# A retention and DeltaNet layer on one core: gate weights in tiles of their own on POOL's queue, an early bias, x in 1 KB packets, a shorter end

## The chip, the core and the metric

The kernel runs on one core of a Trainium2 chip. The engines are PE (TensorE, matmuls), DVE (VectorE), ACT (ScalarE), POOL (GpSimd) and SP (SyncE, which here only issues DMA transfers); SP and POOL each own a queue of transfers, and 16 DMA engines serve both. The metric is device time in microseconds: the median of three runs was 3312.75 (3312.17 to 3316.98). A separately profiled execution gives the trace.

## The reference

One layer with two groups of heads, over 128 context tokens and 256 latent tokens, model width D = 4096, all in float32. Cut to what matters here (the mixer with its scans is left out):

```
mod = silu(c) @ w_ada + b_ada            # w_ada (4096, 3 * 4096)
shift, scale, gate = split(mod, 3)       # one row for the context, one for the latents
u = rms_norm(h, norm_w) * (1 + scale) + shift
out = mixer(u, ...)                      # u @ w_in, retention and gated delta rule, mixed @ w_out
h = h + gate * out
y = rms_norm(h, final_norm_w)
```

The change touches four places: loading x for the first norm, computing `gate`, loading w_out (4096 x 4096), and the last norm with its stores.

## The kernel before

The 384 tokens are three units of 128. A weight tile in fp32 is split into a high and a low part in a narrower float (`split_tile`): ACT casts it (L219, `wh`), DVE subtracts (L220, `wl`). A product is three matmuls: high x high, low x high, high x low (L270 to L272, L276 to L278).

**Start.** SP loads x in 16 blocks of 256 columns for three units, 48 transfers (`xload`, L485), between loads of w_ada. A block's tile holds two halves of 128 columns, each with three units side by side (L480), so a row of 256 columns lands in two places. ACT and DVE sum squares; `xnorm` makes the scale; `uprep` transposes x and applies scale and shift. Then the input projection starts, in stages.

**Middle.** Input projection and mixers, unchanged here. Of the 4096 gate columns, 2560 are computed there on PE.

**Output projection.** Eight groups of 512 columns, each 32 pieces of one 128-row block of w_out. w_out comes in tiles of two pieces from a ring of four (`raw`, RAW_RING), two transfers per tile (L207). The order of the program is written by `run_pieces`: it prepares pieces up to RING - 1 = 4 ahead of the one whose matmuls it writes, so casts and subtractions stand that far ahead on ACT and DVE; pieces of other kinds are written where they stand between.

Between the pieces of groups 1 to 6 stand those of `GateSum`: the last 1536 gate columns, four sums of 384 columns. A piece loads two 128-row blocks of w_ada into a tile of the same `raw` ring by SP (L352); DVE multiplies each block by silu(c) per row and adds it to two accumulators (L360, L362), one per kind of token; the second block's adds are put off behind the next split (`later`). At a sum's end PE adds over partitions (L382), the bias is read into an accumulator by POOL (L386), DVE adds (L388) and POOL writes gate rows to DRAM (L390).

For each group `pre`, five pieces before the group's end, has POOL read the gate rows (`go`, L1356), the last norm's weights (`wo`, L1357) and x (`xo`, L1359, three units), 1.5 MB in all. `rest` forms gate * out, adds x, multiplies by the norm's weight into `hw` and has ACT sum the squares (L1367 to L1372), small steps that are written between the next group's matmuls. The tiles of this stage come from a pool (`op`) that `open_out` opens near the end of group 0, when the mixers' pools are closed.

**End.** After a unit's last group `final` adds the eight sums, takes the inverse root on POOL, scales `hw` in four parts on DVE and ACT in turn (L1338, L1336), and SP stores each (L1339).

Each engine runs its instructions in the order in which they were written; so does each queue of transfers issue them.

Of the kernel before, what the change touches and what calls it, by code (L numbers as in the profile page):

```python
# [7 lines left out]
F32 = mybir.dt.float32  # L8
F32R = mybir.dt.float32r
AF = mybir.ActivationFunctionType  # L10
# [59 lines left out]
def hybrid_step(ctx: ExitStack, tc: tile.TileContext, x_prompt, x_sample, state_ret_fwd, state_ret_bwd,  # L70
# [129 lines left out]
    def load_piece(src, chunks, k0, nk, ring=None):  # L200
        shape = [128, nk, len(chunks), chunks[0][1]]
        if ring:
            raw = ring(shape)
        else:
            raw = wpool.tile(shape, F32, tag="raw", name="raw", bufs=RAW_RING)
        for i, (c0, cn) in enumerate(chunks):
            SP.dma_start(out=raw[:, :, i, :],  # L207
                         in_=src[k0 * 128:(k0 + nk) * 128, c0:c0 + cn].rearrange("(k p) n -> p k n", p=128))
        return raw

    later = []

    def split_tile(raw, shape, place=None):
        if place:
            h, lo = place
        else:
            h = wpool.tile(shape, F32R, tag="wh", name="wh", bufs=RING)
            lo = wpool.tile(shape, F32R, tag="wl", name="wl", bufs=RING)
        A.copy(h, raw)  # L219
        V.tensor_tensor(lo, raw, h.bitcast(F32), op=ALU.subtract)  # L220
        if later:
            later.pop(0)()
        return h, lo

    class Gemm:
# [115 lines left out]
    class GateSum:  # L341
# [3 lines left out]
        slots = 0.0  # L345

        def __init__(self, c0):
            self.c0 = c0
            self.pieces = [(self, i) for i in range(0, NK, 2)]

        def prepare(self, i):
            raw = load_piece(w_ada, [(2 * D + self.c0, GATE_W)], i, 2)  # L352
            if i == 0:
                self.acc = [oc["sb"].tile([128, GATE_W], F32, tag=f"ga{v}", name="gacc", bufs=2) for v in range(2)]

            def add(q):
                for v, acc in enumerate(self.acc):
                    w = cst[:, 2 * (i + q) + v:2 * (i + q) + v + 1]
                    if i + q == 0:
                        V.tensor_scalar(acc, raw[:, q, 0], scalar1=w, scalar2=None, op0=ALU.mult)  # L360
                    else:
                        V.scalar_tensor_tensor(out=acc, in0=raw[:, q, 0], scalar=w, in1=acc, op0=ALU.mult, op1=ALU.add)  # L362
            while later:
                later.pop(0)()
            add(0)
            if i + 2 < NK:
                later.append(lambda: add(1))
            else:
                add(1)

        def compute(self, i, hl):
            if i + 2 == NK:
                urgent.append(self.fin())
            return 1

        def fin(self):
            n, sb = GATE_W // 2, self.acc[0]
            parts = [(32 * q, q // 2, n * (q % 2)) for q in range(4)]
# [5 lines left out]
            for r, v, o in parts:  # L384
# [3 lines left out]
            V.tensor_tensor(sb[:, 0:n], ps, sb[:, 0:n], op=ALU.add)  # L388
            for r, v, o in parts:
                G.dma_start(out=d_gate[v:v + 1, self.c0 + o:self.c0 + o + n], in_=sb[r:r + 1, 0:n])  # L390
            clock["gate"] = self.c0 + GATE_W

    class Do:

# [921 lines left out]
    def open_out():  # L1316
        bg_drain()
        mx_ctx.close()
        mid_ctx.close()
        oc["sb"] = ctx.enter_context(tc.tile_pool(name="op", bufs=1))  # L1320
        oc["ps"] = ctx.enter_context(tc.tile_pool(name="ps_out", bufs=1, space=PSUM))
        oc["hw"] = oc["sb"].tile([128, 3, D], F32, name="hw")
        oc["sq"] = oc["sb"].tile([128, 3, 8], F32, name="sq")
        oc["rstd"] = oc["sb"].tile([128, 3], F32, name="rstd")

    def final(n):

        hw, r = oc["hw"], oc["rstd"][:, n:n + 1]
        V.tensor_reduce(r, oc["sq"][:, n], axis=AX.X, op=ALU.add)
        V.tensor_scalar(r, r, scalar1=1.0 / D, scalar2=EPS, op0=ALU.mult, op1=ALU.add)  # L1330
        power(r, r, 0)
        yield
        for i in range(4):
            cs = slice(1024 * i, 1024 * i + 1024)
            if i % 2:
                A.activation(hw[:, n, cs], hw[:, n, cs], AF.Copy, scale=r)  # L1336
            else:
                V.tensor_scalar(hw[:, n, cs], hw[:, n, cs], scalar1=r, scalar2=None, op0=ALU.mult)  # L1338
            SP.dma_start(out=y_unit[n][:, cs], in_=hw[:, n, cs])  # L1339
            if i % 2:  # L1340
                yield

    def out_done(c0):
        box = {}
        cs = slice(c0, c0 + 512)

        def pre():
            if not oc:
                open_out()
            bg_drain(("out", c0 - 512))  # L1350
            op = oc["sb"]
            assert clock["gate"] >= c0 + 512
            box["x"] = op.tile([128, 3, 512], F32, tag="xo", name="xo", bufs=1)
            box["g"] = op.tile([128, 2, 512], F32, tag="go", name="go")
            box["w"] = op.tile([128, 512], F32, tag="wo", name="wo")
            G.dma_start(out=box["g"], in_=d_gate[:, cs].partition_broadcast(128))  # L1356
            G.dma_start(out=box["w"], in_=final_norm_w[cs].partition_broadcast(128))  # L1357
            for m in range(3):
                G.dma_start(out=box["x"][:, m], in_=x_unit[m][:, cs])  # L1359

        def done(n, ps):
            bg_list.append((("out", c0), rest(n, ps)))

        def rest(n, ps):
            yield
            t = oc["sb"].tile([128, 512], F32, tag="to", name="to", bufs=3)
            V.tensor_tensor(t, ps, box["g"][:, min(n, 1)], op=ALU.mult)  # L1367
            yield
            V.tensor_tensor(t, t, box["x"][:, n], op=ALU.add)
            yield  # L1370
            V.tensor_tensor(oc["hw"][:, n, cs], t, box["w"], op=ALU.mult)
            A.activation(t, t, AF.Square, accum_out=oc["sq"][:, n, c0 // 512:c0 // 512 + 1])  # L1372
            yield
            if c0 + 512 == D:
                yield from final(n)
        return pre, done

# [83 lines left out]
```

## Time and profile before

| what | value |
|---|---|
| median of three runs | 3312.75 us |
| profiled execution, its own time | 3315.79 us |
| its span, first to last instruction | 3313.8 us |
| PE busy | 3217.4 us, 97% of the span |
| DVE busy | 1961.7 us, 59% |
| ACT busy | 1200.1 us, 36% |
| POOL busy | 302.3 us, 9% |
| mean granted clock of PE | 0.987 |
| read from HBM, written | 590.75 MB, 32.33 MB |

A busy PE is not PE at its peak: its instructions overlap, and 512-column matmuls follow each other every 0.23 us, or every 0.43 us where the granted clock is 0.5 (from 2825 us on, for one). Rows of the waits name the waiting engine, its tile and line, whom it waited for, and then the total in us, the number of waits and the longest. Rows of a timeline begin with start and duration in us; in brackets stands the idle time before, and what ended it. "x2" is a number of instructions. A row of DMA issues gives the size of one and the median time to its landing.

### The profile page before, as it was taken

The numbers are of one execution on the slowest core, as the hardware profiler recorded it, in microseconds if no ns is written. First come the engines' busy times: TensorE is split into PE (matmuls) and PEld (weight loads), VectorE is DVE, ScalarE is ACT, GpSimd is POOL, SyncE is SP. The second block draws the span as 40 slices with busy tenths as digits, with TensorE's granted clock in tenths as the row PEclk, the third lists the DMA queues.
The fourth block names the chain that finished last, engine by engine and source line by source line (L and its number), as shares of the span: only waits on it lengthen the run. The fifth ranks groups of instructions, "written<-read, shape, count | busy, mean of one in ns | idle before, by whom it ended". The sixth has DMA issues, their size and how long they took to land.

```text
span 3313.8 us, 51416 instructions
## 1 busy us (share of the span) xinstructions
PE 3217.4 (97%) x18948; PEld 2698.1 (81%) x18948; DVE 1961.7 (59%) x4065; ACT 1200.1 (36%) x2582; POOL 302.3 (9%) x484
## 2 busy tenths in 40 slices
PE   4999999999999999999999999999999999999998
PEld 2778888878799789789898789789789887787876
DVE  2554443336955746745856746756745855766774
ACT  3322222224345245235345245245245345223233
POOL 0000000001011011001011011011001012010001
PEclk7999999999999999999999999999999999999999
DMA  9998998984434644645445645644645445776665
GB/s 295 297 297 262 333 300 273 291 267 137 121 118 127 188 138 151 188 135 153 134 135 154 189 123 160 187 137 141 188 125 156 132 122 183 215 213 199 213 214 171
DMA packets 586941, 626.51 MB, mean 189 GB/s; under 512 B 39642, under 2 KB 569746, under 8 KB 586688
## 3 DMA queue, kind: packets, MB, share of 16 engines
q1 hardware_dynamic: 562160, 551.04, 53.6%
q0 software_dynamic: 24528, 72.18, 7.4%
q8 instruction: 149, 2.44, 0.3%
q14 instruction: 104, 0.85, 0.1%
HBM read 590.75 MB, written 32.33 MB: 188 GB/s over the span
## 4 chain that ended last, share of the span: by engine, by line
PE 80%; DMA 7%; DVE 5%; issue 4%; ACT 2%; POOL 1%; SPq 1%; ACTq 0%; POOLq 0%; DVEq 0%
PE mm L276 12%; PE mm L277 11%; PE mm L278 11%; PE mm L270 10%; PE mm L272 9%; PE mm L271 9%; PE ada L334 3%; DMA raw<-in_w_in_dram 2%; PE o L277 2%; PE o L276 2%; PE o L278 2%; DVE wl L220 2%; DMA raw<-in_w_out_dram 2%; PE adg L334 1%; DMA mixl<-d_mix 1%
## 5 line engine op out<-in xcount | busy, mean ns | idle before, releaser
L220 DVE TENSOR_TENSOR wl<-raw,wh 128x512 fp32r<-128x512 f32 x1274 | 853.7, 686 | 800.0 <-ACT wh L219 792.9
L219 ACT CAST wh<-raw 128x512 fp32r<-128x512 f32 x1274 | 757.0, 620 | 1327.0 <-DMA raw<-in_w_in_dram 524.6
L276 PE MATMUL mm<-wh,uh 128*128 128x512 f32 x1920 | 772.7, 402 | 6.8 <-ACT wh L219 4.1
L277 PE MATMUL mm<-wl,uh 128*128 128x512 f32 x1920 | 750.4, 391 | 1.3 <-DVE wl L220 1.3
L278 PE MATMUL mm<-wh,ul 128*128 128x512 f32 x1920 | 749.9, 391 | 0.0
L270 PE MATMUL mm<-uh,wh 128*128 128x384 f32 x2048 | 723.2, 353 | 6.6 <-DVE ul L618 3.2
L272 PE MATMUL mm<-uh,wl 128*128 128x384 f32 x2048 | 687.0, 335 | 0.1
L271 PE MATMUL mm<-ul,wh 128*128 128x384 f32 x2048 | 686.5, 335 | 0.0
L276 PEld LDWEIGHTS mm<-wh,uh 128*128 128x128 f32 x1920 | 361.1, 188 | 120.8 <-issue 36.3
L270 PEld LDWEIGHTS mm<-uh,wh 128*128 128x128 f32 x2048 | 386.4, 189 | 53.2 <-issue 37.8
L278 PEld LDWEIGHTS mm<-wh,ul 128*128 128x128 f32 x1920 | 361.1, 188 | 78.0 <-DVE ul L1313 0.3
L277 PEld LDWEIGHTS mm<-wl,uh 128*128 128x128 f32 x1920 | 361.7, 188 | 72.3 <-DVE wl L220 3.3
L271 PEld LDWEIGHTS mm<-ul,wh 128*128 128x128 f32 x2048 | 386.7, 189 | 4.5 <-issue 3.3
L272 PEld LDWEIGHTS mm<-uh,wl 128*128 128x128 f32 x2048 | 385.7, 188 | 0.6 <-DVE wl L220 0.4
L917 DVE TENSOR_TENSOR tmp<-M 48x4 f32<-48x4 f32 (+14 forms) x240 | 190.3, 793 | 5.2
L334 PE MATMUL ada<-adar,cst 128*32 128x256 f32 x2048 | 148.5, 405 | 28.5 <-DMA adar<-in_w_ada_dram 28.3
L708 DVE SCALAR_TENSOR_TENSOR acc<-rawt,cw,acc 128x126 f32<-128x126 f32 (+3 forms) x384 | 134.0, 410 | 26.8 <-ACT acc L703 26.8
L362 DVE SCALAR_TENSOR_TENSOR gacc<-raw,cst,gacc 128x384 f32<-128x384 f32 x248 | 141.1, 611 | 9.1 <-DMA raw<-in_w_ada_dram 9.1
L277 PE MATMUL o<-wl,uh 128*128 128x512 f32 x354 | 140.1, 396 | 4.2 <-DVE wl L220 4.1
L276 PE MATMUL o<-wh,uh 128*128 128x512 f32 x354 | 140.2, 396 | 3.7 <-ACT wh L219 3.7
L278 PE MATMUL o<-wh,ul 128*128 128x512 f32 x354 | 139.5, 394 | 0.0
L334 PEld LDWEIGHTS ada<-adar,cst 128*32 128x32 f32 x2048 | 53.5, 112 | 95.4 <-DMA adar<-in_w_ada_dram 45.8
(329 smaller groups left out, 2616.7 us busy)
## 6 DMA issues: line engine op xcount, KB each, us to landing
raw<-in_w_in_dram SPq DMA_DIRECT2D x1028, 256.0 KB, 3.6
adar<-in_w_ada_dram SPq DMA_DIRECT2D x256, 512.0 KB, 6.0
raw<-in_w_out_dram SPq DMA_DIRECT2D x256, 256.0 KB, 3.8
raw<-in_w_ada_dram SPq DMA_DIRECT2D x80, 512.0 KB, 4.2
raw<-in_w_ada_dram SPq DMA_DIRECT2D x64, 384.0 KB, 4.2
rawt<-d_part POOLq DMA_DIRECT2D x26, 384.0 KB, 6.1
d_part<-spill POOLq DMA_DIRECT2D x9, 768.0 KB, 7.1
gr<-d_gc POOLq DMA_DIRECT2D x16, 384.0 KB, 7.4
```

The lines of the kernel that those rows point to most:

```text
L219: A.copy(h, raw)
L220: V.tensor_tensor(lo, raw, h.bitcast(F32), op=ALU.subtract)
L270: PE.matmul(ps, wh, high(k), start=st, stop=False)
L271: PE.matmul(ps, wh, low(k), start=False, stop=False)
L272: PE.matmul(ps, wl, high(k), start=False, stop=sp)
L276: PE.matmul(ps, a, h, start=st, stop=False)
L277: PE.matmul(ps, a, lo, start=False, stop=False)
L278: PE.matmul(ps, b, h, start=False, stop=sp)
L334: PE.matmul(self.ps[32 * q:32 * q + 32, cs], cst[:, 2 * k:2 * k + 32], raw[:, q, 0], start=(k < 4), stop=(k >= NK - 4), tile_position=(0, ...
L362: V.scalar_tensor_tensor(out=acc, in0=raw[:, q, 0], scalar=w, in1=acc, op0=ALU.mult, op1=ALU.add)
L708: V.scalar_tensor_tensor(out=dst[:, lo:hi], in0=x[:, lo + o:hi + o], scalar=w(t), in1=dst[:, lo:hi], op0=ALU.mult, op1=ALU.add)
L917: V.tensor_tensor(t, M[0:48, 0:i, 0:i].rearrange("p j c -> p c j"), M[0:48, i:i + 1, 0:i].to_broadcast([48, i, i]), op=ALU.mult)
```

## The change

Four edits:

1. `GateSum` works on one 128-row block per piece (128 pieces in place of 64), in tiles `graw` of its own (two, 192 KB each) that POOL loads. Its adds stand directly behind the load in the program; `later` is gone. The bias gets a tile of its own, `gbias`, and is read halfway through the sum. The store of the gate rows follows DVE's sum two steps after the matmuls.
2. `load_piece` reads two adjacent chunks as one, which holds for w_out: one transfer of 512 KB with rows of 2 KB per tile in place of two.
3. A block's x tile is laid out by unit first, so that a row's 256 columns land in one place.
4. In `final` the sum over seven of the eight parts is made before the last group's product is read, the last square writes into PSUM instead of over its input, and the first 1024 columns are scaled and stored in two halves. The ring `to` has two tiles in place of three.

```
+        if len(chunks) == 2 and chunks[1][0] == sum(chunks[0]):
+            c0, cn = chunks[0]
+            SP.dma_start(out=raw.rearrange("p k i n -> p k (i n)"),
+                         in_=src[k0 * 128:(k0 + nk) * 128, c0:c0 + 2 * cn].rearrange("(k p) n -> p k n", p=128))
+            return raw
...
-            self.pieces = [(self, i) for i in range(0, NK, 2)]
+            self.pieces = [(self, k) for k in range(NK)]
...
-            raw = load_piece(w_ada, [(2 * D + self.c0, GATE_W)], i, 2)
+            raw = oc["sb"].tile([128, GATE_W], F32, tag="graw", name="graw", bufs=2)[:, 0:self.width]
+            G.dma_start(out=raw, in_=w_ada[k * 128:k * 128 + 128, c0:c0 + self.width])
...
+            if k == NK // 2:
+                self.bias = oc["sb"].tile([128, GATE_W // 2], F32, tag="gb", name="gbias")[:, 0:self.width // 2]
+                for r, v, o in self.parts:
+                    G.dma_start(out=self.bias[r:r + 32], in_=b_ada[0, c0 + o:c0 + o + self.width // 2].partition_broadcast(32))
...
-            for r, v, o in parts:
-                c0 = 2 * D + self.c0 + o
-                G.dma_start(out=sb[r:r + 32, 0:n], in_=b_ada[0, c0:c0 + n].partition_broadcast(32))
-            yield 2000
-            V.tensor_tensor(sb[:, 0:n], ps, sb[:, 0:n], op=ALU.add)
+            V.tensor_tensor(sb, ps, sb, op=ALU.add)
...
-    xs = [pair("uh", m, F32).rearrange("p k (n c) -> p k n c", n=3) for m in range(NK // 2)]
+    xs = [pair("uh", m, F32).rearrange("p k t -> p (k t)").rearrange("p (n k c) -> p k n c", n=3, k=2)
+          for m in range(NK // 2)]
...
-        V.tensor_reduce(r, oc["sq"][:, n], axis=AX.X, op=ALU.add)
-        V.tensor_scalar(r, r, scalar1=1.0 / D, scalar2=EPS, op0=ALU.mult, op1=ALU.add)
+        V.tensor_scalar(r, oc["sq"][:, n, 7:8], scalar1=1.0 / D, scalar2=oc["part"][:, n:n + 1], op0=ALU.mult, op1=ALU.add)
...
-        for i in range(4):
-            cs = slice(1024 * i, 1024 * i + 1024)
+        for eng, c0, cn in ((V, 0, 512), (A, 1024, 1024), (V, 512, 512), (V, 2048, 1024), (A, 3072, 1024)):
+            cs = slice(c0, c0 + cn)
...
+            last = c0 + 512 == D
+            if last:
+
+                part = oc["part"][:, n:n + 1]
+                V.tensor_reduce(part, oc["sq"][:, n, 0:7], axis=AX.X, op=ALU.add)
+                V.tensor_scalar(part, part, scalar1=1.0 / D, scalar2=EPS, op0=ALU.mult, op1=ALU.add)
+            t = oc["sb"].tile([128, 512], F32, tag="to", name="to", bufs=2)
...
-            A.activation(t, t, AF.Square, accum_out=oc["sq"][:, n, c0 // 512:c0 // 512 + 1])
+            A.activation(ps if last else t, t, AF.Square, accum_out=oc["sq"][:, n, c0 // 512:c0 // 512 + 1])
```

How this moves the order of instructions, at three places. First POOL's queue from the end of group 0 on (mixl: the last rows of the mixers' output; go, wo, xo as above; gacc and d_gate: bias and gate rows), before:

```order
L1309 DMA mixl<-d_mix_119 128x384
L1356 DMA go<-d_gate 128x2x512
L1357 DMA wo<-in_final_norm_w_dram 128x512
L1359 DMA xo<-in_x_prompt_dram 128x512
L1359 DMA xo<-in_x_sample_dram 128x512 x2
```

and in the changed kernel:

```order
L1305 DMA mixl<-d_mix_119 128x384
L1350 DMA go<-d_gate 128x2x512
L1351 DMA wo<-in_final_norm_w_dram 128x512
L1353 DMA xo<-in_x_prompt_dram 128x512
L1353 DMA xo<-in_x_sample_dram 128x512 x2
L356 DMA graw<-in_w_ada_dram 128x384 x17
L363 DMA gbias<-in_b_ada_dram 32x192 x4
L356 DMA graw<-in_w_ada_dram 128x384 x4
L1350 DMA go<-d_gate 128x2x512
```

Where before the next group's reads followed at once, 21 gate loads and a bias now stand between, and the first gate load stands behind the first burst of reads.

Second DVE at the same place, in the changed kernel (wl: subtractions; gacc: the gate's adds; to: the group's product read and x added):

```order
L223 TENSOR_TENSOR wl<-raw,wh 128x512
L367 TENSOR_SCALAR gacc<-graw,cst 128x384 x2
L223 TENSOR_TENSOR wl<-raw,wh 128x512
L369 SCALAR_TENSOR_TENSOR gacc<-graw,cst,gacc 128x384 x2
L1367 TENSOR_TENSOR to<-mm_25543,go 128x512
L1369 TENSOR_TENSOR to<-to,xo 128x512
L223 TENSOR_TENSOR wl<-raw,wh 128x512 x2
```

These rows stand as they did before, but for the name: the adds read graw where they read raw.

Third POOL's queue later, where a store of gate rows stands close behind a burst, in the changed kernel:

```order
L356 DMA graw<-in_w_ada_dram 128x384 x15
L1350 DMA go<-d_gate 128x2x512
L1351 DMA wo<-in_final_norm_w_dram 128x512
L1353 DMA xo<-in_x_prompt_dram 128x512
L1353 DMA xo<-in_x_sample_dram 128x512 x2
L356 DMA graw<-in_w_ada_dram 128x384 x3
L385 DMA d_gate<-gbias 16x1x12 x4
L356 DMA graw<-in_w_ada_dram 128x384 x14
```

Before, POOL had nothing but such bursts, biases and stores here; now each has gate loads behind it. On SP the projection's 256 loads of w_out with 64 of w_ada between them become 128 of w_out alone.

More of the change, by code (lines that the diff above doesn't have):

```diff
@@ L347, in __init__ @@
         def __init__(self, c0):
-            self.c0 = c0
-            self.pieces = [(self, i) for i in range(0, NK, 2)]
-        def prepare(self, i):
-            raw = load_piece(w_ada, [(2 * D + self.c0, GATE_W)], i, 2)
[L353 to L369, printed above, removed]
+            self.c0, self.width = c0, min(GATE_W, D - c0)
@@ new lines, in __init__, with prepare @@
+            self.parts = [(32 * q, q // 2, self.width // 2 * (q % 2)) for q in range(4)]
+            self.pieces = [(self, k) for k in range(NK)]
+        def prepare(self, k):
+            c0 = 2 * D + self.c0
+            raw = oc["sb"].tile([128, GATE_W], F32, tag="graw", name="graw", bufs=2)[:, 0:self.width]
+            G.dma_start(out=raw, in_=w_ada[k * 128:k * 128 + 128, c0:c0 + self.width])
+            if k == 0:
+                self.acc = [oc["sb"].tile([128, GATE_W], F32, tag=f"ga{v}", name="gacc", bufs=2)[:, 0:self.width]
+                            for v in range(2)]
+            if k == NK // 2:
+                self.bias = oc["sb"].tile([128, GATE_W // 2], F32, tag="gb", name="gbias")[:, 0:self.width // 2]
+                for r, v, o in self.parts:
+                    G.dma_start(out=self.bias[r:r + 32], in_=b_ada[0, c0 + o:c0 + o + self.width // 2].partition_broadcast(32))
+            for v, acc in enumerate(self.acc):
+                w = cst[:, 2 * k + v:2 * k + v + 1]
+                if k == 0:
+                    V.tensor_scalar(acc, raw, scalar1=w, scalar2=None, op0=ALU.mult)
+                else:
+                    V.scalar_tensor_tensor(out=acc, in0=raw, scalar=w, in1=acc, op0=ALU.mult, op1=ALU.add)
@@ L376, in fin @@
         def fin(self):
-            n, sb = GATE_W // 2, self.acc[0]
-            parts = [(32 * q, q // 2, n * (q % 2)) for q in range(4)]
+            n, sb = self.width // 2, self.bias
             yield GATE
             ps = ps_main.tile([128, n], F32, tag="mm3", name="gsum")
-            for r, v, o in parts:
+            for r, v, o in self.parts:
                 PE.matmul(ps[r:r + 32], ones, self.acc[v][:, o:o + n], start=True, stop=True, tile_position=(0, r))
             yield
-            for r, v, o in parts:
-                c0 = 2 * D + self.c0 + o
-                G.dma_start(out=sb[r:r + 32, 0:n], in_=b_ada[0, c0:c0 + n].partition_broadcast(32))
-            yield 2000
[L388 to L391, printed above, removed]
+            V.tensor_tensor(sb, ps, sb, op=ALU.add)
+            for r, v, o in self.parts:
+                G.dma_start(out=d_gate[v:v + 1, self.c0 + o:self.c0 + o + n], in_=sb[r:r + 1])
+            clock["gate"] = self.c0 + self.width
     class Do:
@@ L1371, in rest @@
             V.tensor_tensor(oc["hw"][:, n, cs], t, box["w"], op=ALU.mult)
[L1372 removed]
+            A.activation(ps if last else t, t, AF.Square, accum_out=oc["sq"][:, n, c0 // 512:c0 // 512 + 1])
             yield
[L1374 removed]
+            if last:
                 yield from final(n)
```

11 lines of the change are left out of this document (3 added, 8 removed).

## The prediction

> **What bounds the kernel now.** I read the chain of waits first, then the windows of the stage that the change touches most, then who waits for whom there.
>
> ```profile
> span 3313.8 us, 51416 instructions
> PE 80%; DMA 7%; DVE 5%; issue 4%; ACT 2%; POOL 1%; SPq 1%; ACTq 0%; POOLq 0%; DVEq 0%
> ```
>
> TensorE (PE) holds 80% of the chain, and the change removes no matmul. Time can only come from stretches where PE waits or runs at a lowered clock: the start, which waits for DMA, the output projection (2811 to 3299 us), and the end after the last matmul. The next view is windows of PE in the projection: stretch, length, PE busy, granted clock, DMA share, GB/s.
>
> ```profile
> 2811.00:2830.00 19.00, 15.18 (x58) 0.91 0.66 181
> 2830.00:2846.00 16.00, 14.45 (x55) 0.89 0.75 226
> ...
> 2965.00:2990.00 25.00, 22.36 (x88) 0.93 0.67 206
> ...
> 3045.00:3065.00 20.00, 18.37 (x76) 1.00 0.72 217
> 3065.00:3172.00 107.00, 107.00 (x478) 1.00 0.69 215
> 3172.00:3198.00 26.00, 22.43 (x88) 0.93 0.71 199
> ```
>
> Between the troubled stretches PE is full (107.00 of 107.00). Stretches two, three, four and six lose 1.55 + 2.64 + 1.63 + 3.57 = 9.4 us idle, and by the clock 16 x 0.11 + 25 x 0.07 + 26 x 0.07 = 5.3 us more: **14.7 us**. The first stretch is another matter (below). Who is waited for from 2846 to 3240 us, first by SP's DMA queue, then by the engines (total, times, longest):
>
> ```profile
> SPq L207 <- DVE gacc L362: 135.0, 35, 8.3
> ```
>
> ```profile
> ACT wh L219 <- DMA raw<-in_w_out_dram: 106.7, 32, 9.1
> ...
> DVE gacc L388 <- DMA gacc<-in_b_ada_dram: 9.0, 4, 3.0
> ```
>
> ScalarE (ACT) waits for w_out that landed late. SP could not issue it earlier: it stood at a ring tile that VectorE (DVE) still used for gate weights. And DVE stood 3 us at each bias.
>
> **The change, part by part.**
>
> *x in 1 KB packets: -4.5 us.* The chain at the start runs through x's last landing to the first projection matmuls:
>
> ```profile
> 50.47 3.08 DMA uh<-in_x_sample_dram
> ...
> 55.20 0.90 POOL rx L140
> ...
> 63.01 0.44 PE mm L272
> ```
>
> The DMA view for four stretches: 12 to 15 us (x alone, 512 B packets; with the queue's share of 16 engines), 54 to 76 and 92 to 110 us (nearly all 1 KB), and 4 to 54 us (both):
>
> ```profile
> DMA packets 1605, 0.78 MB, mean 259 GB/s; under 512 B 98, under 2 KB 1605, under 8 KB 1605
> ...
> q1 hardware_dynamic: 1605, 0.78, 104.3%
> ```
>
> ```profile
> DMA packets 7463, 7.77 MB, mean 353 GB/s; under 512 B 286, under 2 KB 7397, under 8 KB 7461
> ```
>
> ```profile
> DMA packets 5778, 5.72 MB, mean 318 GB/s; under 512 B 226, under 2 KB 5776, under 8 KB 5776
> ```
>
> ```profile
> DMA packets 22078, 15.31 MB, mean 306 GB/s; under 512 B 1111, under 2 KB 22044, under 8 KB 22075
> ```
>
> 16 engines for 3 us over 1605 packets are 29.9 ns a packet; for 22 us over 7463 they are 47.2 ns. x is 48 transfers of 256 packets, 12,288; as 6,144 of 1 KB each pair saves 2 x 29.9 - 47.2 = 12.6 ns, over 16 engines 4.8 us. By rate instead, 15.31 MB at 353 GB/s take 43.4 us of the 50: 6.6 us, the upper bound. By 5778 packets in 18 us, 49.8 ns each, it is 3.8, the lower bound. I take 4.5. All behind it waits on x or on a full DMA (353 GB/s from 54 us), so the rest shifts with it.
>
> The Trainium skill ("DMA: Bandwidth & Descriptors", Specifications) names 512 B as the smallest transfer at line rate; by it x would gain nothing and the sum be 4.5 us smaller. The x-only slice, its engines full (104.3%) at 259 GB/s against 353, speaks against that rule.
>
> *w_out alone in the ring, one transfer a tile: returns 12 us of the 14.7.* A piece of w_out takes 2.04 us, from the casts when nothing is late:
>
> ```profile
> 3010.92 0.62 ACT L219 CAST wh<-raw 128x512 fp32r<-128x512 f32 x1 [1.42 <-PE o L278]
> 3012.96 0.62 ACT L219 CAST wh<-raw 128x512 fp32r<-128x512 f32 x1 [1.42 <-PE o L278]
> ```
>
> Before, 4 ring tiles were shared by 96 w_out and 64 gate tiles, 2.4 for w_out: from the release of a tile to its next use 3.8 pieces or 7.8 us. After it is 7 pieces, 14.3 us, more than the longest wait of 9.1. So the ACT waits go. The 128 fewer SP issues are worth nothing by themselves: SP waits for tiles, not for its own time.
>
> *Gate weights on POOL: 0 in steady flow.* 192 KB each, 128 loads, two tiles; DVE's adds come as pairs:
>
> ```profile
> 3005.18 1.14 DVE L362 SCALAR_TENSOR_TENSOR gacc<-raw,cst,gacc 128x384 f32<-128x384 f32 x2
> ```
>
> Two gate pieces stand beside three w_out pieces, 6.12 us; a load starts when the adds two pieces back are done and must land 6.12 - 1.14 = 4.98 us later. The nearest row is POOL's load of a 128x384 tile (mixl) beside the same splits:
>
> ```profile
> DMA to landing us min/median/max: 2.6/3.3/5.1
> ```
>
> 3.3 fits, 5.1 misses by 0.1. What hides a miss: the splits run 4 pieces ahead of PE, 8.2 us less 1.3 for cast and subtraction, 6.9 us.
>
> *What stands in the same queue.* Every group, POOL first reads gate rows, norm weights and x (go, wo, xo; 1.5 MB), and a gate load is now behind them. The DMA view from 2846 to 3240 us (last column: us to landing), and rows of POOL's timeline:
>
> ```profile
> xo<-in_x_sample_dram POOLq DMA_DIRECT2D x10, 256.0 KB, 9.3
> ```
>
> ```profile
> 2813.34 0.71 POOL L1356 DMA_DIRECT2D go<-d_gate  x1 [4.52 <-PE mm L278]
> ...
> 2815.14 1.07 POOL L1359 DMA_DIRECT2D xo<-in_x_sample_dram  x2
> ...
> 3032.54 1.98 POOL L390 DMA_DIRECT2D d_gate<-gacc  x4 [3.29 <-DVE gacc L388]
> ```
>
> Issuing the five takes 2.87 us; a load behind them lands about 0.54 + 2.87 + 8.7 = 12.1 us after the one before was issued, where 3 x 3.06 - 1.14 = 8.0 is due: DVE 4.1 us late, six times, under the 6.9. A store of gate rows (1.98 us, behind DVE's sum) makes the next load 1.98 + 3.3 + 0.5 after the preceding adds where 1.9 is due: 3.9 late, four times. One store follows a burst by three gate loads: 4.1 + 3.9 - 6.9 = 1.1 us on PE, with lowered clock 2.7. That is why 12 of 14.7. Bounds: 0 and 14.7.
>
> *The bias, fetched 16 pieces early.* DVE's four 3 us waits go; the four fetches (2 us of POOL, as the store) fall between loads. Counted in the 12.
>
> *The first group's end: +6 us.* The gate tiles exist only once the output pool is open, so the first loads are issued behind the first go, wo and xo, while their adds keep their place on DVE ahead of two subtractions. Before, the gate weights were there by then. DVE, then PE:
>
> ```profile
> 2814.14 0.67 DVE L220 TENSOR_TENSOR wl<-raw,wh 128x512 fp32r<-128x512 f32 x1
> ...
> 2820.08 0.69 DVE L1367 TENSOR_TENSOR to<-mm,go 128x512 f32<-128x512 f32 x1 [4.22 <-DMA go<-d_gate]
> 2822.64 0.69 DVE L1369 TENSOR_TENSOR to<-to,xo 128x512 f32<-128x512 f32 x1 [1.87 <-DMA xo<-in_x_prompt_dram]
> 2823.25 1.29 DVE L220 TENSOR_TENSOR wl<-raw,wh 128x512 fp32r<-128x512 f32 x2
> ```
>
> ```profile
> 2823.99 0.80 PE L277 MATMUL o<-wl,uh 128*128 128x512 f32 x1 [3.68 <-DVE wl L220]
> ```
>
> The last xo is issued at 2815.7 and lands at 2825.0; the gate load behind it soon after, say 2825.3. Then DVE has to do two adds (0.9), a subtraction (0.67), two adds (1.1), L1367 and L1369 (1.4), a subtraction (0.65): 2830 in place of 2823.9. Bounds: 0, if the load lands 3.3 us after its issue at 2816.2, before go; 8, if it takes 2 us longer. The clock's recovery afterwards is paid in both kernels. I take 6.
>
> *The end: -1.2 us.* The timeline behind the last matmul:
>
> ```profile
> 3301.34 0.69 DVE L1371 TENSOR_TENSOR hw<-to,wo 128x512 f32<-128x512 f32 x1
> 3302.07 0.63 ACT L1372 ACTIVATE to<-to 128x512 f32<-128x512 f32 x1 [2.84 <-DVE hw L1371]
> ...
> 3302.82 0.16 DVE L1329 TENSOR_REDUCE rstd<-sq 128x1 f32<-128x8 f32 x1 [0.79 <-ACT to L1372]
> 3303.02 0.15 DVE L1330 TENSOR_SCALAR rstd<-rstd 128x1 f32<-128x1 f32 x1
> ...
> 3303.83 1.41 DVE L1338 TENSOR_SCALAR hw<-hw,rstd 128x1024 f32<-128x1024 f32 x2 [0.66 <-POOL rstd L140]
> ```
>
> The square wrote where L1371 reads, and so waited for it: into PSUM it starts 0.73 us earlier. The sum over seven of the eight parts is made ahead, so the step of 0.20 at 3302.82 goes. Scaling 1024 columns takes DVE 0.7 (1.41 for two), so a first store of 512 starts about 0.35 earlier, but the next waits for ACT's 1024 columns: I count 0.27 for it. Bounds 0.8 and 1.6.
>
> **Sum.** -4.5 - 12 + 6 - 1.2 = **-11.7 us**. The profiled execution took 3315.79 us (span 3313.8 and 2.0 around it) and becomes 3304.1; it lies 3.0 us above the median of the three runs, 3312.75, which so becomes **3301**. A difference under 0.2% (6.6 us) can't be told from none here.
>
> **Rivals.** *A, the lead is spent (0.16, no change).* If DVE meets a burst with its lead mostly used, since L1367 to L1371 of three units fall in the same place, half of the 4.1 us reaches PE six times: 12.3 us, 3313. For it: those operations are 6.2 us in 8 pieces. Against: PE is full for 107 us at a time.
>
> *B, the gate loads set the pace (0.07, slower).* It decides once a load takes over 4.9 us with DVE's start: then two gate pieces take the loading time plus 1.24 us. This row is for POOL loads of double the size:
>
> ```profile
> rawt<-d_part POOLq DMA_DIRECT2D x26, 384.0 KB, 6.1
> ```
>
> At 6.1 us, two pieces take 7.34 instead of 6.12, 64 times 1.22: +78 us, 3379. Against it: the 3.3 of the equal tile. The Trainium skill ("SBUF — State Buffer", two separate sides) has a rule for it: POOL's transfers wait for descriptors while VectorE runs a two-port operation, 620 ns becoming 3100. With those 2.5 us on 3.3 the loads would miss the 4.9. But it excepts operations with two inputs like these splits and adds, and the 3.3 was measured beside such splits.
>
> *C, x gains nothing (0.08):* 3305.5, if other work than DMA sets the start. Against: DMA is full there.
>
> *D, the first loads do not wait for the burst (0.13):* 3295.
>
> That the gate weights have no queue of their own, only one shared with these bursts, is in the forecast already.
>
> **Numbers.** Forecast 0.56, A 0.16, B 0.07, C 0.08, D 0.13. Low: -6.6 - 14.7 + 0 - 1.6 gives 3290, both extremes at once, so 3291; high: A with some of the gain, 3311. Left out are B, a part of A and little more. Faster by over 0.2%: the forecast but 0.03 of it, D, and 0.07 of C, 0.73; within: those pieces and 0.14 of A, 0.18; slower: B and 0.02 of A, 0.09.
>
> **What would show it.** x: its last landing near 49 us in place of 53.5. The first group's end: a PE wait for a subtraction near 10 us where 3.7 stood, with DVE waiting for graw. After it: hardly an ACT wait on w_out, no DVE wait at the bias, some 4 us of DVE waiting at graw behind each xo, and PE full but for one stretch. The end: the square beside L1371. I am wrong if DVE waits for graw in steady flow, or if PE idles at every group's end again.

## The result: slower, by 0.4 to 0.5%

| | before | changed |
|---|---|---|
| first comparison, median (us) | 3312.92 | 3335.34 |
| ratio, 95% interval | | 1.0054 (1.0039 to 1.0068) |
| repeated later, median (us) | 3317.99 | 3330.50 |
| ratio, 95% interval | | 1.0039 (1.0026 to 1.0053) |
| profiled execution, span (us) | 3313.8 | 3329.9 |

One execution of 5989 us in the first comparison was disturbed and is left out. The forecast was 3301, faster; by the ratios the changed kernel needs 13 to 18 us more than before instead of 12 less (the medians of the first comparison lie 22 us apart, those of the second 12.5). In the two profiled executions the difference is 15.9 us (3331.68 against 3315.79).

The chain of waits of the changed kernel: TensorE's share falls from 80 to 76%, and DMA's rises from 7 to 10.

```profile
span 3329.9 us, 51321 instructions
PE 76%; DMA 10%; issue 5%; DVE 4%; POOL 2%; ACT 2%; SPq 0%; ACTq 0%; POOLq 0%; DVEq 0%
```

Who PE waits for from 2790 to 3310 us, before and then changed (total, times, longest):

```profile
PE o L277 <- DVE wl L220: 4.1, 3, 3.7
PE mm L276 <- ACT wh L219: 4.1, 3, 3.1
PE o L276 <- ACT wh L219: 3.7, 2, 2.3
PE mm L277 <- DVE wl L220: 1.1, 5, 0.2
```

```profile
PE o L278 <- DVE wl L223: 15.6, 8, 9.0
PE mm L278 <- DVE wl L223: 5.3, 8, 2.6
PE mm L277 <- ACT wh L222: 2.2, 4, 0.7
PE o L277 <- ACT wh L222: 1.7, 3, 0.8
```

13.0 us of waiting became 25.2 (0.4 of it in a row that is not shown), and 20.9 of it is for DVE's subtraction. What ACT and DVE wait for in the changed kernel, from 2845 to 3280 us:

```profile
ACT wh L222 <- PE o L279: 105.1, 72, 2.8
ACT wh L222 <- PE mm L279: 100.1, 68, 3.4
```

```profile
DVE gacc L369 <- DMA graw<-in_w_ada_dram: 90.9, 63, 7.7
DVE wl L223 <- ACT wh L222: 33.4, 33, 1.4
```

So the wait that the change was to remove is gone: ACT's casts waited 106.7 us for w_out before, and now they wait for PE, as they should. No wait at the bias is left either. In its place DVE waits 90.9 us for gate weights ahead of the second and later products of a sum, the longest 7.7.

**One group's reads in detail.** POOL's timeline, then DVE's, then PE's, around the reads of 2955 us:

```profile
2954.72 0.54 POOL L356 DMA_DIRECT2D graw<-in_w_ada_dram  x1 [2.39 <-DVE gacc L369]
2955.25 0.73 POOL L1350 DMA_DIRECT2D go<-d_gate  x1
...
2957.06 1.06 POOL L1353 DMA_DIRECT2D xo<-in_x_sample_dram  x2
2958.11 0.54 POOL L356 DMA_DIRECT2D graw<-in_w_ada_dram  x1
```

```profile
2958.33 1.15 DVE L369 SCALAR_TENSOR_TENSOR gacc<-graw,cst,gacc 128x384 f32<-128x384 f32 x2 [1.04 <-DMA graw<-in_w_ada_dram]
2959.40 1.28 DVE L223 TENSOR_TENSOR wl<-raw,wh 128x512 fp32r<-128x512 f32 x2
2968.38 1.15 DVE L369 SCALAR_TENSOR_TENSOR gacc<-graw,cst,gacc 128x384 f32<-128x384 f32 x2 [7.69 <-DMA graw<-in_w_ada_dram]
2969.44 0.68 DVE L223 TENSOR_TENSOR wl<-raw,wh 128x512 fp32r<-128x512 f32 x1
```

```profile
2966.99 0.39 PE L277 MATMUL o<-wh,uh 128*128 128x512 f32 x1
2970.18 0.50 PE L278 MATMUL o<-wl,uh 128*128 128x512 f32 x1 [2.80 <-DVE wl L223]
...
2971.84 0.73 PE L278 MATMUL o<-wl,uh 128*128 128x512 f32 x1 [0.69 <-DVE wl L223]
2972.37 0.63 PE L279 MATMUL o<-wh,ul 128*128 128x512 f32 x1
```

And the transfers issued from 2958.0 to 2959.5 us (last column: us from issue to landing):

```profile
xo<-in_x_sample_dram POOLq DMA_DIRECT2D x1, 256.0 KB, 9.9
graw<-in_w_ada_dram POOLq DMA_DIRECT2D x1, 192.0 KB, 10.2
```

DVE was done at 2960.69 and sat until 2968.38. PE ran dry at 2967.38 (2966.99 + 0.39): its lead was 2967.38 - 2960.69 = 6.7 us, as forecast (6.9). But when the load came, an add pair and a subtraction (1.7 us) still stood before what PE waits for: 7.69 + 1.7 - 6.7 = 2.7, and the row shows 2.80. Then eight matmuls ran at some 0.63 us instead of 0.39. That the 6.7 agrees with the forecast is chance, as the experiment with w_out in halves shows.

**Where the 16 us are.** I add up, in every profiled execution, how far each matmul's start lies beyond 0.227 us after the one before it, from 2785 us to the last matmul: PE's lost time in the projection. It holds the waits and the slowed matmuls behind them.

| kernel | lost in the projection | in it, around the first group's end (2805 to 2845) | waits alone |
|---|---|---|---|
| before | 25.2 | 9.8 | 13.0 |
| changed | 38.7 | 12.0 | 25.2 |
| changed, profiled again | 41.7 | 11.5 | 24.6 |

13.5 of the 15.9 us are here. Ahead of the projection the changed kernel's execution stood 3 us late from 1000 us on and 5 at 2800 us; the end gave 2.6 back.

### The profile page after: what moved, and what is told of

Same layout as the page of the kernel before. It is cut to its first block, busy times and chain, and to the rows that moved or that the text cites. A ratio compares the mean times of both kernels' runs of the same rounds, so it can differ in the third digit from the quotient of the medians.

```text
span 3329.9 us, 51321 instructions
## 1 busy us (share of the span) xinstructions
PE 3224.1 (97%) x18948; PEld 2704.2 (81%) x18948; DVE 1962.9 (59%) x4071; ACT 1202.1 (36%) x2582; POOL 370.7 (11%) x612
## 3 DMA queue, kind: packets, MB, share of 16 engines
q0 software_dynamic: 32720, 97.35, 10.4%
## 4 chain that ended last, share of the span: by engine, by line
PE 76%; DMA 10%; issue 5%; DVE 4%; POOL 2%; ACT 2%; SPq 0%; ACTq 0%; POOLq 0%; DVEq 0%
PE mm L277 11%; PE mm L278 10%; PE mm L271 10%; PE mm L279 10%; PE mm L273 10%; PE mm L272 10%; DMA graw<-in_w_ada_dram 5%; PE ada L335 3%; DMA adar<-in_w_ada_dram 2%; DMA raw<-in_w_in_dram 1%; PE adg L335 1%; PE o L278 1%; PE o L279 1%; DVE wl L223 1%; PE o L277 1%
## 5 line engine op out<-in xcount | busy, mean ns | idle before, releaser
L369 DVE SCALAR_TENSOR_TENSOR gacc<-graw,cst,gacc 128x384 f32<-128x384 f32 x248 | 141.8, 613 | 91.2 <-DMA graw<-in_w_ada_dram 90.9
L278 PE MATMUL o<-wl,uh 128*128 128x512 f32 x354 | 140.2, 396 | 15.6 <-DVE wl L223 15.6
```

The costliest lines, as they stand in the source:

```text
L278: PE.matmul(ps, a, lo, start=False, stop=False)
L369: V.scalar_tensor_tensor(out=acc, in0=raw, scalar=w, in1=acc, op0=ALU.mult, op1=ALU.add)
```

## The experiments

A difference in us is the ratio's distance from 1, times 3316. The ratio is the one on record for the two sets of executions, and not always the quotient of the medians beside it.

### x in 1 KB packets alone

```diff
-    xs = [pair("uh", m, F32).rearrange("p k (n c) -> p k n c", n=3) for m in range(NK // 2)]
+    xs = [pair("uh", m, F32).rearrange("p k t -> p (k t)").rearrange("p (n k c) -> p k n c", n=3, k=2)
+          for m in range(NK // 2)]
```

> The kernel before with x in 1 KB packets and nothing else. The prediction's own term says -4.5 us (bounds -3.8 to -6.6), so 3308 us beside a before of 3313. The rival, read from the trace after (x landed 3.4 us earlier, the first product began only 0.9 us earlier, and 15 us later nothing of it was left), says that another load is last there: 3312 to 3314, no difference. If the new layout itself costs the 3 to 5 us by which the changed kernel is late from 300 us on, 3316 to 3318.

Measured: 3313.73 against 3315.05; ratio 0.9995 (0.9986 to 1.0004), -1.7 us (-4.6 to +1.3). The forecast's -4.5 is at the interval's edge; the rival of the expectation (3312 to 3314) holds. The chain of waits at the start of this kernel:

```profile
44.73 4.05 DMA uh<-in_x_prompt_dram
...
50.07 9.03 DMA adar<-in_w_ada_dram
...
59.14 0.64 PE ada L334 x8
59.78 0.47 PE mm L270
```

The landing of x in this chain, at 48.78, is not the last: the last of the 48 transfers lands at 49.51, before at 53.55 (50.47 + 3.08). That is 4.0 us sooner, where the arithmetic by packets gave 4.8. In the eleven profiled kernels with the new x the last one lands at 49.5 to 51.6 us, 50.5 in the mean, in the three with the old x at 52.7 to 53.7, 53.3 in the mean: 2.8 us. Then the chain changes over to a load of the modulation weights (adar) that lands at 59.10, and the first projection matmul is 2.3 us earlier than before (59.71 against 62.06 in the two profiles; 0.9 us in the means of the eleven and the three). What is left of it 250 us on can't be seen in single profiles: the eleven kernels with the new x do the same work up to 2780 us, and at the same cast near 1004 us they stand from 8.3 us ahead of before to 4.7 behind it, 0.3 behind in the mean; the three with the old x, before among them, 0 to 3.5 behind.

### The new gate sums alone

```diff
-            raw = load_piece(w_ada, [(2 * D + self.c0, GATE_W)], i, 2)
+            raw = oc["sb"].tile([128, GATE_W], F32, tag="graw", name="graw", bufs=2)[:, 0:self.width]
+            G.dma_start(out=raw, in_=w_ada[k * 128:k * 128 + 128, c0:c0 + self.width])
...
```

> The kernel before with the new gate sums alone (tiles of their own, POOL's queue, early bias); x, the halves of w_out's loads and the end as before. The theory that the gate sums make the whole loss (DVE waits 7.7 us for the load behind each group's reads, the tensor engine's lead is 6.9 us): 3323 to 3335, 10 to 22 us above before, and some 12 us more of tensor engine idle time between 2785 and 3300 us. The prediction's account (-14.7 of stalls returned as 12, +6 at the opening): about 3305. The rival that the loss comes from x or the merged w_out transfer: 3313 or less.

Measured: 3322.28; ratio 1.0019 (1.0009 to 1.0029), +6.3 us; lost in the projection 28.4. So the gate sums lose by themselves, but less than the whole change, and less than this expectation's low end. (The ring `to` has two tiles here as well. It has them with five gate tiles too, where nearly nothing is lost behind the first group, so it is not the cause.) x does not lose (above). That leaves the end and the merged transfer.

### The shorter end alone

```diff
-        V.tensor_reduce(r, oc["sq"][:, n], axis=AX.X, op=ALU.add)
-        V.tensor_scalar(r, r, scalar1=1.0 / D, scalar2=EPS, op0=ALU.mult, op1=ALU.add)
+        V.tensor_scalar(r, oc["sq"][:, n, 7:8], scalar1=1.0 / D, scalar2=oc["part"][:, n:n + 1], op0=ALU.mult, op1=ALU.add)
...
-            A.activation(t, t, AF.Square, accum_out=oc["sq"][:, n, c0 // 512:c0 // 512 + 1])
+            A.activation(ps if last else t, t, AF.Square, accum_out=oc["sq"][:, n, c0 // 512:c0 // 512 + 1])
```

> The kernel before with the shorter end alone. The prediction's sum for it is -1.2 us (bounds -0.8 to -1.6); the trace after suggests -2.6, since POOL's last drain also ended sooner there. 3311 to 3314 beside 3314 to 3315; if the end is what loses, above 3317.

Measured: 3317.25 against 3317.99; ratio 1.0000 (0.9990 to 1.0009): too small to show in the time. In the profile the last unit's product with go (L1367's instruction) begins 13.86 us before the span's end in the kernel before, 13.00 here: -0.86.

### w_out in halves again, and the changed kernel once more

```diff
-        if len(chunks) == 2 and chunks[1][0] == sum(chunks[0]):
-            c0, cn = chunks[0]
-            SP.dma_start(out=raw.rearrange("p k i n -> p k (i n)"),
-                         in_=src[k0 * 128:(k0 + nk) * 128, c0:c0 + 2 * cn].rearrange("(k p) n -> p k n", p=128))
-            return raw
         for i, (c0, cn) in enumerate(chunks):
```

> The changed kernel with w_out's pieces loaded as two transfers of 256 KB each again instead of one of 512 KB. If the merged transfer is what makes the change lose 15 us more than the gate sums alone (gate loads between larger w_out transfers, each later by a little), 3320 to 3324. If the merge is neutral, as the prediction had it (its cost was put at nothing), the same as the changed kernel, 3333 to 3338.

> The changed kernel once more, unaltered, beside the three below on one chip. 3332 to 3339 as first measured; this fixes the base, since the new gate sums alone cost only 7 us and x nothing, so that some 15 us of the 24 are without an owner.

Measured, on one chip: halves 3323.19, ratio 1.0018 (1.0010 to 1.0027); changed kernel 3330.50, ratio 1.0039 (1.0026 to 1.0053). The merge costs about 7 us, as the first side of the expectation had it; the repeat itself came out below the 3332 expected. PE's waits with the halves:

```profile
PE o L273 <- DVE wl L218: 12.4, 9, 9.4
PE mm L273 <- DVE wl L218: 2.5, 7, 0.8
```

Without the first group's stall, 12.4 - 9.4 + 2.5 = 5.5 us of waiting for DVE are left where the changed kernel has 15.6 - 9.0 + 5.3 = 11.9. The first gate load behind the reads of groups two to six landed 9.5, 10.2, 11.7, 11.2 and 9.8 us after its issue in the changed kernel (10.7, 10.1, 11.7, 11.4 and 9.5 when repeated) and 9.3, 9.2, 10.4, 10.1 and 9.2 with the halves: 0.8 to 1.0 us sooner in the mean. The landing is only a part of it. The table gives, at each of these groups, DVE's wait behind the reads; the lead, from the moment DVE stops to the first matmul that needs its next subtraction (PE's own wait taken off); and that matmul's stall.

| wait, lead, stall (us) | group 2 | 3 | 4 | 5 | 6 |
|---|---|---|---|---|---|
| changed | 6.2, 8.9, 0 | 7.7, 6.7, 2.8 | 7.5, 10.4, 0 | 7.6, 7.2, 2.2 | 7.4, 6.7, 2.6 |
| w_out in halves | 5.9, 8.9, 0 | 6.8, 8.1, 0.6 | 5.9, 9.6, 0 | 7.9, 9.0, 0.6 | 6.5, 8.9, 0 |
| three tiles (below) | 3.7, 8.9, 0 | 3.8, 8.9, 0 | 1.9, 9.6, 0 | 2.6, 8.9, 0 | 3.5, 8.9, 0 |

With three tiles, where DVE's waits are short, the lead is 8.9 us (9.6 at group 4, where a new sum begins): I call that a full lead. The changed kernel stalls where it met the reads with 6.7 to 7.2, at three of the five groups, and there the halves have 1.4 to 2.2 us more of lead. Why the merge delays the loads and shortens the lead is not settled. (The expectation for the repeat counted 15 us without an owner; with 12.9 for the whole, 7 for the merge and 6 for the gate sums, none is left; but the 7 is itself taken from this repeat.)

### The group's reads on SP's queue

```diff
-            G.dma_start(out=box["g"], in_=d_gate[:, cs].partition_broadcast(128))
+            SP.dma_start(out=box["g"], in_=d_gate[:, cs].partition_broadcast(128))
...
```

The reads of wo and xo go to SP in the same way.

> The changed kernel with the group's reads (go, wo, xo) issued on SP's queue instead of POOL's, so that a gate load no longer stands behind them in its queue. If the place in the queue makes the load take 10.2 us instead of 3.3, the load after each group's reads lands in 3 to 5 us, DVE's long waits go and 8 to 13 us come back: 3324 to 3329 beside 3337. If it is that the bytes share the 16 DMA engines, whichever queue issues them, the long waits stay at 7 us or more and the time stays within 3 us of 3337.

Measured: 3320.58, ratio 1.0019 (1.0009 to 1.0030): 7 to 12 us better than the changed kernel. Transfers issued from 2933.5 to 2939 us:

```profile
graw<-in_w_ada_dram POOLq DMA_DIRECT2D x3, 192.0 KB, 7.4
go<-d_gate SPq DMA_DIRECT2D x1, 512.0 KB, 10.4
xo<-in_x_sample_dram SPq DMA_DIRECT2D x2, 256.0 KB, 10.8
```

The gate loads have POOL's queue to themselves and still take 7 to 9 us (8.0, 8.8, 9.1, 8.8 and 9.1 for the slowest at groups two to six). So the place in the queue is a part, near 2 us of the 7 by which the load is late (10.5 against 3.4 in steady flow), and the bytes in flight at the same time are the rest: neither side of the expectation is right alone. And w_out's loads now stand behind reads that wait for their tiles at the first group's end:

```profile
PE o L277 <- ACT wh L222: 12.5, 4, 10.0
```

### A third of the reads' bytes

```diff
-            G.dma_start(out=box["w"], in_=final_norm_w[cs].partition_broadcast(128))
-            for m in range(3):
-                G.dma_start(out=box["x"][:, m], in_=x_unit[m][:, cs])
+            if c0 == 0:
+                G.dma_start(out=box["w"], in_=final_norm_w[cs].partition_broadcast(128))
+                for m in range(3):
+                    G.dma_start(out=box["x"][:, m], in_=x_unit[m][:, cs])
```

The first group's two tiles are kept and used by all eight.

> The changed kernel (two tiles, one queue) that reads wo and xo for the first group alone and uses them for all eight, so that the outputs are wrong and each later group reads 512 KB (go) instead of 1.5 MB. If the bytes in front of the gate load make it late, it lands in about 5 to 7 us there instead of 9.5 to 11.7, DVE's slip falls below the tensor engine's lead, and all that is lost behind the first group comes back: 3314 to 3320 beside 3330, the stall at the first group's end staying. If five issues on POOL's queue or the two tiles in steady flow make the loss, 3326 or more.

Measured: 3306.19, ratio 0.9967 (0.9957 to 0.9977), better than expected. PE's waits, and DVE's from 2845 to 3280 us:

```profile
PE o L278 <- DVE wl L223: 9.7, 2, 9.5
```

```profile
DVE gacc L369 <- DMA graw<-in_w_ada_dram: 65.7, 59, 4.8
```

DVE still waits 59 times, up to 4.8 us, and PE hardly feels it: 5.1 us are lost outside the first group's end. The load behind the reads takes 7.1, 6.0, 5.5, 5.9 and 6.1 us. Two tiles and one queue carry the gate weights well enough; it is the reads ahead of one load in each group that cost. This run takes away two things together: 1 MB ahead of the load, and the 2.1 us in which POOL issues it. With that gone the change comes out 10.9 us ahead of before (in a kernel that reads less, so not one to use).

### Three tiles and five

```diff
-            raw = oc["sb"].tile([128, GATE_W], F32, tag="graw", name="graw", bufs=2)[:, 0:self.width]
+            graw["n"] += 1
+            m = graw["n"] % 5
+            if m < 3:
+                raw = oc["hw"][:, m, D - GATE_W:D - GATE_W + self.width]
+            else:
+                raw = oc["sb"].tile([128, GATE_W], F32, tag="graw", name="graw", bufs=2)[:, 0:self.width]
```

The third to fifth tiles lie in hw's last columns, which are idle until the last group writes them. For three tiles the rule is `% 3` and `m < 1`.

> The changed kernel with five gate weight tiles instead of two (three of them lie in columns of hw that the last group alone writes), same queue and same program order. Three more pieces of lead are about 15 us, more than the 7.7 us that the load behind the group's reads is late: if late gate loads make the tensor engine's stalls, they go at every group but the first, 10 to 13 us: 3324 to 3328. If the loss lies ahead of the projection (start and middle), nothing changes: 3334 to 3338.

> The changed kernel with three gate weight tiles (the third in columns of hw that the last group alone writes). A load behind the group's reads takes 8.3 to 11.7 us, and each tile more is one piece, some 4 to 5 us, more of lead. If lateness against lead is the whole account, three tiles leave DVE 3 to 5 us late, less than the tensor engine's lead of 6.9: the stalls at the five later groups go nearly as with five tiles, 3304 to 3310. If every us of DVE's waiting counts (91 us of waits in all), the gain lies half way between two tiles (3330) and five (3303), 3314 to 3320.

Measured: five 3302.93, ratio 0.9962 (0.9948 to 0.9975); three 3305.71, ratio 0.9970 (0.9957 to 0.9983). PE's waits with five, then with three:

```profile
PE o L278 <- DVE wl L223: 9.2, 2, 9.0
PE o L277 <- ACT wh L222: 0.9, 1, 0.9
```

```profile
PE o L278 <- DVE wl L223: 9.7, 2, 9.5
```

Nothing is left but the stall at the first group's end. The loads behind the reads land as late as ever (9.7, 10.3, 10.3, 8.6 and 11.2 us with five tiles), so it is lateness against lead, as the first side of the expectation for three tiles had it (3304 to 3310): one tile more takes 2.5 to 5.6 us off DVE's waits (the table above), which decides, and the fourth and fifth add next to nothing. I had expected 10 to 13 us off the changed kernel from five tiles and got 26 to 31, since I had not counted that all of the return on w_out (below) was still hidden behind those stalls.

### Five tiles with w_out in halves

> Five gate weight tiles and w_out again in two transfers a piece. With two tiles the halves brought 7 us (late gate loads landed 0.9 us sooner at each group). With five tiles no gate load is late, so the merge should not matter: a ratio of 0.995 to 0.998, as with five tiles alone (0.9962). If the merge costs by itself, 0.994 or less.

Measured: 3302.71, ratio 0.9962 (0.9949 to 0.9976), equal to five tiles alone. The merge costs only where a late gate load reaches PE.

### The first group's end

```diff
-            pieces += interleave(behind, gate_sums) + gm.pieces
+            pieces += behind[:8] + interleave(behind[8:], gate_sums) + gm.pieces
```

> The changed kernel with five gate weight tiles, and the first gate sum begun eight pieces later, so that no gate load stands behind the first group's reads. The stall of 9.2 us at the first group's end is then gone with its slow matmuls behind it: 6 to 11 us less than five tiles alone (3302.9), 3292 to 3297. If the stall only moves to the next wait (w_out's loads or the reads themselves are late there), 3300 to 3304.

Measured: 3306.83 against 3317.99, ratio 0.9964 (0.9951 to 0.9977): no gain over five tiles. DVE and PE at that place:

```profile
2821.31 0.69 DVE L1374 TENSOR_TENSOR to<-mm,go 128x512 f32<-128x512 f32 x1 [7.02 <-DMA go<-d_gate]
```

```profile
2825.27 0.50 PE L278 MATMUL o<-wl,uh 128*128 128x512 f32 x1 [4.65 <-DVE wl L223]
```

The stall moved to the next wait in DVE's order: the product with go, behind which two subtractions stood. So that product had to move as well:

```diff
         def rest(n, ps):
-            yield
+            yield 9000 if c0 == n == 0 else None
```

> The same with the first gate sum begun eight pieces later and the first group's products with go held back some 12 us, so that nine subtractions stand ahead of the reads' landing on DVE. Without this the stall only moved from the gate load to go (4.8 us and 1.6 us). If it now goes, 4 to 8 us below five tiles alone: a ratio of 0.9938 to 0.9955. If it moves to the next wait again (w_out's own loads landing late beside the reads), 0.996.

Measured: 3292.21 (3290.50 to 3294.07) against 3316.69, ratio 0.9927 (0.9915 to 0.9940): 24 us faster than before, and the best of all kernels here. It is 11.6 us below five tiles alone, more than the 4 to 8 expected; 6.9 to 8.6 of it are in PE's lost time (table below), the rest has no owner. The product was not moved by itself, so what it does without the later gate sums is not shown. PE's two largest waits over the whole projection, and its busy time in two windows of it:

```profile
PE o L272 <- ACT wh L217: 1.6, 2, 0.8
PE mm L273 <- DVE wl L218: 0.7, 3, 0.2
```

```profile
2780.00:2845.00 65.00, 64.15 (x286) 52.68 (x284) 37.45 (x64) 24.68 (x49) 16.06 (x30) 1.00 0.72 222
2845.00:3270.00 425.00, 422.77 (x1875) 345.67 (x1875) 303.38 (x520) 136.92 (x247) 99.55 (x186) 1.00 0.68 207
```

PE is busy for 486.9 of 490 us at full clock, and loses 6.6 us in the projection.

PE's lost time in all of them, from the profiled executions:

| kernel | lost in the projection | around the first group's end | ratio to before |
|---|---|---|---|
| before | 25.2 | 9.8 | 1 |
| x alone | 21.7 | 8.4 | 0.9995 |
| end alone | 24.4 | 7.4 | 1.0000 |
| gate sums alone | 28.4 | 10.9 | 1.0019 |
| changed | 38.7 and 41.7 | 12.0 and 11.5 | 1.0054 and 1.0039 |
| w_out in halves | 29.2 | 12.0 | 1.0018 |
| reads on SP | 33.8 | 16.3 | 1.0019 |
| a third of the reads | 18.9 | 13.8 | 0.9967 |
| three tiles | 15.9 | 13.8 | 0.9970 |
| five tiles | 15.2 | 13.2 | 0.9962 |
| five tiles, halves | 13.5 | 11.6 | 0.9962 |
| five tiles, later sums | 14.5 | 8.5 | 0.9964 |
| five tiles, halves, later sums and products | 6.6 | 1.5 | 0.9927 |

## Why the prediction was wrong, point by point

**x, -4.5: sooner, but by less, and the path was not it.** x landed 4.0 us sooner in this edit's profile and 2.8 in the mean of all, where the sum had 4.8 by packets and 3.8 as its lower bound. "All behind it waits on x or on a full DMA" is the step of this term that failed: a load of adar landed last, and the whole is -1.7 (-4.6 to +1.3). That is rival C, or near it. The Trainium skill ("DMA: Bandwidth & Descriptors", Specifications) has 512 B as enough for line rate, by which nothing would be gained. The time nearly agrees; the landing (49.51 against 53.55) does not, so the rule gives the right answer here for another reason than the one that the runs show.

**w_out alone in the ring, -12 of 14.7: right, but not in the kernel as changed.** Outside the first group's end PE lost 25.2 - 9.8 = 15.4 us before. With five tiles it loses 15.2 - 13.2 = 2.0: 13.4 came back, and of ACT's 106.7 us of waiting on w_out 0 to 7.1 are left in the kernels with the new gate sums. In the changed kernel itself 38.7 - 12.0 = 26.7 are lost there, so the return is used up and 11.3 us more.

**The reads in the same queue: the step that failed.** I put DVE 4.1 us late behind each group's reads, six times, "under the 6.9", at no cost but one coincidence with a store. DVE was 7.7 us late at the group shown, and 6.2 to 7.6 at the other four. Of the 3.6 between, 1.5 is the landing (13.6 us after the issue of the load before, 2968.28 - 2954.72, where I had 12.1), from too small an estimate for a load behind 1.5 MB. And 2.0 is DVE itself: I let it come 8.0 us after that issue, at the steady pace of three pieces, while it came at 2960.69, after 6.0: on its way there it waited only once, 1.04 us for the load before, and was not held to that pace. On top I set the lateness against the lead bare. The add pair and the subtraction of 1.7 us that follow the late load come off the lead too. 7.7 + 1.7 against 6.7 is a stall; 4.1 against 6.9 was none.

The lead itself was no fixed number either. Full, it is 8.9 us and not 6.9, and 7.7 + 1.7 against 8.9 is half a microsecond; in the changed kernel it was down to 6.7, 7.2 and 6.7 at the three groups where PE stalled. At two of these three a store of gate rows stands 16 to 18 us ahead of the reads, and DVE had waited 5.0 us (at 2945) and 4.4 (at 3157) for the gate load behind it. I had counted one meeting of a store with the reads, for 2.7. What else used up the lead is not worked out. So rival A, the lead already spent when the reads come, is what happened at these groups, by other work than the one that it named. It had half of the lateness reach PE, which would have made 3313; more than that did, with the slowed matmuls behind the stalls. As the sum stood on a margin of 2.8 us, crossed six times, its bound of 0 for the gain was too kind: a loss belonged in the range.

**The merge, at nothing: wrong.** It costs 7 us beside two tiles and nothing beside five. I had asked only whether SP's issues matter, not whether 512 KB in one piece delays others.

**Gate weights in steady flow, 0: right for the landing, not shown for the lead.** Median 3.4 us to landing, as the 3.3 I took. But my own sign of being wrong, DVE waiting for graw in steady flow, did come: of the 63 waits in the changed kernel 53 are of 2 us or less, 0.8 in the mean. With a third of the reads such waits cost PE little by themselves. What they take from the lead ahead of a late load is not worked out. Rival B (the loads set the pace) did not come. The rule of the Trainium skill that I set beside it ("SBUF — State Buffer", two separate sides) foresees POOL's transfers held up by VectorE's two-port operations, but not by `tensor_tensor` with its two inputs, as the splits are; the 3.4, beside such splits, agrees with the exception.

**The bias, nothing left of its wait: right.** **The first group's end, +6: right in mechanism, too large as time.**

```profile
2830.03 0.75 DVE L367 TENSOR_SCALAR gacc<-graw,cst 128x384 f32<-128x384 f32 x2 [11.19 <-DMA graw<-in_w_ada_dram]
```

```profile
2831.43 0.79 PE L278 MATMUL o<-wl,uh 128*128 128x512 f32 x1 [9.04 <-DVE wl L223]
```

PE's stall grew from 3.68 to 9.04, by 5.4. The time lost around it grew by less: by 2.2 up to 2845 us (12.0 against 9.8), by 3.7 up to 2860 (13.6 against 9.9). A second stall behind it had cost 1.33 us and seven slow matmuls before; in the changed kernel it is 0.71 us without them, and lies at 2849.7, outside the table's window. I had counted that second stall among the 14.7 of w_out, so the two terms overlap. That removing the stall at this place needed both the gate sums and the product with go to move, I had not seen.

**The end, -1.2: right in mechanism, near the lower bound of 0.8, and not seen in the time.** The changed kernel's rows:

```profile
3320.13 0.60 ACT L1372 ACTIVATE o<-to 128x512 f32<-128x512 f32 x1 [2.97 <-DVE to L1369]
3320.13 0.69 DVE L1371 TENSOR_TENSOR hw<-to,wo 128x512 f32<-128x512 f32 x1
...
3320.88 0.21 DVE L1326 TENSOR_SCALAR rstd<-sq,part 128x1 f32<-128x1 f32 x1
3321.17 0.54 POOL L140 TENSOR_TENSOR rstd<-rstd,half_c 128x1 f32<-128x1 f32 x1 [6.24 <-DVE rstd L1326]
```

The square starts beside the product with wo, and one step is gone. The edit alone is worth 0.86 in its profile, and 1.3 between the gate sums alone (12.51 us from L1367's instruction to the end) and the whole change (11.23). The other 1.35 of the changed kernel's 2.63 comes with the gate sums (last section).

In one sum, against before: x -1.7, the end about -1, the gate sums with w_out in halves +6.3, whose 13.4 of return is more than spent on late loads, and the merge +7: +10.6, where the whole measured +12.9 when repeated. The merge's 7 is taken from that repeat, so what the sum tests is the rest: 3.6, beside 6.0 measured for the kernel with the halves.

## What to carry to other kernels

When a load is moved into a queue with large reads, count the bytes ahead of it and not only its place: the next load behind them lands when they have landed, one on another queue is late as well (7 to 9 us here in place of 3.4), and tiles already filled are what helped. Set that lateness, plus the work that follows the load on the waiting engine, against the lead of the engine behind it, taken where the late load meets it (6.7 to 7.2 us at the groups that stalled, 8.9 when full); where the two are within a few us, give one tile more before anything else (here one of 192 KB, from columns that lay idle, turned +13 us into -10). And when a stall is moved, read the order of the waiting engine down to the next operand that lands late, and move that too.

## What the runs showed of the hardware that I had not expected

- The time that slow matmuls cost behind a stall of PE does not grow with the stall. In the output projection of the 14 profiled kernels 25 of the 29 stalls of 1.33 to 10.0 us were followed by 6 to 14 matmuls that start 0.43 us apart in place of 0.227 (in four cases only after a second stall of 0.7 us close behind the first), 1.4 to 3.0 us more. None of 1.30 us or less that stood alone was followed by more than one. So a stall of 2 us costs about as much again, one of 9 us a fifth or a third of itself, and one under 1.3 us little beyond its length.
- A load of 192 KB that takes 3.4 us in steady flow takes 7 to 9 us beside 1.5 MB of another queue's reads, and 8.6 to 11.7 behind them in its own.
- The same work at the start (up to 1004 us) took up to 13 us more in one execution than in another (-8.3 to +4.7 us against before), and the difference stayed to the end. So an edit of the start worth 4 us is seen in the medians or not at all.
- The end of the run can be POOL's and not the last store's. POOL's closing DRAIN, behind its last power, takes 9.74 us in the kernel before and with the end alone, 1.65 with the gate sums alone and in the changed kernel, and 9.08 with a third of the reads. Its rows in the kernel before and with the gate sums alone (number; shortest, median and longest in ns; first and last start):

```profile
L1457 POOLq DRAIN  x3: 51/103/9740, 3303.2 to 3313.5; - x3
```

```profile
L1447 POOLq DRAIN  x3: 46/103/1655, 3307.9 to 3316.8; - x3
```

  In the kernel before the run ends 0.8 us behind this DRAIN, and the last store has landed 2.6 us ahead of the end; with the gate sums alone the last store lands 1.2 us ahead of it. So the shorter DRAIN brings 1.35 us, and the long one hides part of the shorter end where that stands alone: there the last store lands 1.04 us sooner after L1367's instruction, and the span is 0.86 shorter. What makes the DRAIN long stays open.
